# A hybrid decoder trunk: transposes, grams, merges and the recurrence placed at fixed distances among the projections

## The chip, the core and the metric

One Trainium2 chip, one of its cores. The time is the device time of one execution of the whole program in microseconds, of which a median of several runs is given. The matrix engine is TensorE (PE); VectorE (DVE), ScalarE (ACT) and GpSimd (POOL) work elementwise, and SyncE (SP) issues DMAs. Matmuls write to PSUM, which has eight banks, and the elementwise engines empty it.

## What is computed

A trunk of two layers on a sequence of 1024 tokens and 1024 channels, in float32. Each layer is a mixer and a SwiGLU feed-forward part (FFN), each with a norm before and a residual sum after it:

```python
proj = rms_norm(x, norm1_g) @ w_in                 # q, k, v, z of 4 heads, b, a, and 3 x 512 short-conv columns
qkv = silu(causal_depthwise_conv(qkv, dn_conv_w))
q, k = l2_normalize(q), l2_normalize(k)            # 4 heads of 128
beta, g = sigmoid(b_in), -exp(a_log) * softplus(a_in + dt_bias)
o_dn = chunk_gated_delta_rule(q, k, v, g, beta)    # S_t = a_t S_{t-1} (I - b_t k_t k_t^T) + b_t v_t k_t^T, o_t = S_t q_t
o_dn = rms(o_dn) * dn_norm_g * silu(z)
y = gate_b * causal_depthwise_conv(gate_c * hv, sc_conv_w);  o_sc = rms per group(y) * sc_norm_g
x = x + concatenate([o_dn, o_sc]) @ w_out
x = x + (silu(h2 @ ffn_w_gate) * (h2 @ ffn_w_up)) @ ffn_w_down
```

## The kernel before

Tokens lie along the free axis in two halves of 512, channels on the 128 partitions. Each projection of 128 columns and one half is 24 matmuls of 128x512 (mm3, L179 to 184): 8 blocks of channels, each as high part by high part (L182), high by low (L183) and low by high (L184), so that float32 precision is kept with a faster type. ACT makes the high part of a weight (L175), DVE or POOL the low part (L176). All projections share the two PSUM buffers named mm.

The mixer goes head by head. kvq (L432) projects k, q or v of a head and a half; conv_silu (L410 to 427) runs the convolution and the silu on ACT (L418, L420, L426) and DVE (L424, L427) and leaves kT, qT or vT, channels on the partitions. transposed (L451) turns such a tile with four PE transposes into ktok, qtok or vtok, tokens on the partitions. head_stats takes the sums of squares of ktok and qtok and from them the norms and the factors c2, irk and s. prep (L480 to 517) fetches the decay row of a half by DMA (L487), makes eta and the masked exponentials on ACT and POOL (L489 to 499), multiplies the row by c2 on POOL (L500), kdec by kd on DVE (L501), makes v2 from vtok (L504), and the two grams gk and gq (L513), which with the row give U and A (L514); q by eta is POOL's (L515). invert (DVE, 62 steps) and merge (PE products rp and yp, L543 to 580) invert the triangular blocks of 4 tiles of 128 tokens, as X and Y. chain (L584 to 636) is the recurrence over those tiles for two heads: kS = S times k, rr (DVE), TR = Y times rr, vn (ACT), SU and op. zproj and gate apply the silu gate with a transposition ot. sconv makes a short-convolution group and its transposition sp_sc for the sums of squares. ba projects the columns of beta and decay.

The order of work on each engine is not the written order: a list scheduler places the instructions of all engines by their dependencies and its own model of times, with the written order as a priority. A tile's buffers (the dictionary SB, L69) and PSUM banks limit it: a buffer is free when its last reader is done. The row has one buffer, v one, k and q four; in PSUM ch0, ch1, o0, o1, aux and fx have one bank each, mm two. The driver:

```python
head_stats(hd)
for half in range(2):
    if (hd, half) != (0, 0):
        kvq(hd, half, "v")
    prep(hd, half, slots[hd, half])
```

for each head, then invert and all four merges of the pair of heads, then chain for half 0 and half 1, and behind the first pair z of heads 0 and 1 and sconv(0), behind the second sconv 1 to 3 and z of heads 2 and 3. ktok and the merges use the bank aux; qtok ch0; vtok ch1; gk o0; gq o1; ot ch0 and ch1. In the first layer the second half of x is transposed (xtp1) and normed (bc_n1_0_1) ahead of head 0, L291 to 306.

## Time and profile before

| | us |
|---|---|
| median of 3 runs (2547.13 to 2552.06) | 2549.05 |
| the profiled execution's own time | 2534.03 |
| its span | 2532.3 |
| PE busy in it | 2385.5 |
| DVE busy in it | 1666.4 |
| ACT busy in it | 911.6 |
| POOL busy in it | 770.4 |

The busy times are sums over the whole span and do not say which engine sets the end of a stage. The windows of the trace do: they cut the span into stages and give each engine's busy time and the clock granted to PE in each. Positions are in us from the span's start. A row of the waits says which instruction stood still and whose result it stood for; a row of the timeline gives the start and length of an instruction, with the idle time ahead of it in brackets. Ends of matmuls are modelled, so the distance from one start to the next is the better measure of one.

### The profile page before, as it was taken

How to read it: one execution, taken by the hardware profiler on the slowest of the kernel's cores; microseconds unless marked ns; L12 is line 12 of the kernel's file. 1: busy time of each engine (PE TensorE's matmuls, PEld its weight loads, DVE VectorE, ACT ScalarE, POOL GpSimd, SP SyncE). 2: the span in 40 equal slices, each digit the busy share in tenths (PEclk: the TensorE clock that was granted, in tenths of full speed). 3: DMA queues.
4: the chain of work that ended last, by engine and by line, in shares of the span. 5: the costliest groups of instructions: out<-in, count | busy, mean ns of one | idle time of the engine just before them, and what ended most of it. 6: DMA issues, size and time to landing. Idle time of an engine off the chain costs nothing.

```text
span 2532.3 us, 31892 instructions
## 1 busy us (share of the span) xinstructions
PE 2385.5 (94%) x11522; PEld 1935.4 (76%) x11522; DVE 1666.4 (66%) x2771; ACT 911.6 (36%) x1925; POOL 770.4 (30%) x570
## 2 busy tenths in 40 slices
...
GB/s 219 65 56 61 69 57 76 138 202 72 120 100 104 107 102 90 226 137 132 110 76 71 60 55 66 73 63 212 156 77 93 113 116 92 104 147 176 138 130 67
DMA packets 360085, 274.15 MB, mean 108 GB/s; under 512 B 47310, under 2 KB 293368, under 8 KB 359928
## 3 DMA queue, kind: packets, MB, share of 16 engines
...
## 4 chain that ended last, share of the span: by engine, by line
PE 70%; DVE 12%; issue 6%; DMA 5%; ACT 4%; POOL 2%; SPq 0%; POOLq 0%; ACTq 0%; DVEq 0%
PE P_g L183 5%; PE P_g L184 5%; PE P_g L182 5%; PE P_u L183 5%; PE P_u L182 5%; PE P_u L184 5%; PE P_d L183 3%; PE P_d L182 3%; PE P_d L184 3%; DMA row<-gd 2%; PE po L182 2%; PE po L183 2%; PE po L184 2%; PE ps_hsc L182 1%; PE ps_hsc L183 1%
## 5 line engine op out<-in xcount | busy, mean ns | idle before, releaser
L183 PE MATMUL P_g<-lo_hP,hiP_g 128*128 128x512 f32 x616 | 241.6, 393 | 8.6 <-DVE lo_hP L770 6.7
L182 PE MATMUL P_u<-hi_hP,hiP_u 128*128 128x512 f32 x616 | 241.7, 392 | 6.9 <-ACT hiP_u L794 6.9
L182 PE MATMUL P_g<-hi_hP,hiP_g 128*128 128x512 f32 x616 | 240.5, 391 | 1.3 <-ACT hiP_g L794 1.3
L183 PE MATMUL P_u<-lo_hP,hiP_u 128*128 128x512 f32 x616 | 241.4, 392 | 0.0
L184 PE MATMUL P_u<-hi_hP,loP_u 128*128 128x512 f32 x616 | 241.0, 391 | 0.0
L184 PE MATMUL P_g<-hi_hP,loP_g 128*128 128x512 f32 x616 | 240.1, 390 | 0.0
L183 PE MATMUL P_d<-lo_dP,hiP_d 128*128 128x512 f32 x504 | 203.1, 404 | 16.0 <-POOL lo_dP L770 13.0
L182 PE MATMUL P_d<-hi_dP,hiP_d 128*128 128x512 f32 x504 | 202.4, 403 | 11.6 <-ACT hi_dP L769 9.4
L184 PE MATMUL P_d<-hi_dP,loP_d 128*128 128x512 f32 x504 | 199.5, 397 | 1.8 <-DVE loP_d L795 1.7
L1069 DVE TENSOR_TENSOR xT<-P_d,xT 128x512 f32<-128x512 f32 x192 | 127.0, 681 | 53.9 <-PE P_d L184 50.5
L770 POOL TENSOR_TENSOR lo_hP<-xh,hi_hP 128x512 fp32r<-128x512 f32 x24 | 37.1, 1574 | 403.4 <-ACT hi_hP L769 403.4
L183 PEld LDWEIGHTS P_g<-lo_hP,hiP_g 128*128 128x128 f32 x616 | 116.0, 188 | 38.2 <-DVE lo_hP L770 11.1
L182 PEld LDWEIGHTS P_u<-hi_hP,hiP_u 128*128 128x128 f32 x616 | 116.6, 189 | 32.1 <-ACT hiP_u L794 7.8
L182 PEld LDWEIGHTS P_g<-hi_hP,hiP_g 128*128 128x128 f32 x616 | 115.9, 188 | 26.9 <-ACT hiP_g L794 2.1
L184 PEld LDWEIGHTS P_u<-hi_hP,loP_u 128*128 128x128 f32 x616 | 116.6, 189 | 24.5
L183 PEld LDWEIGHTS P_u<-lo_hP,hiP_u 128*128 128x128 f32 x616 | 116.6, 189 | 24.2
L184 PEld LDWEIGHTS P_g<-hi_hP,loP_g 128*128 128x128 f32 x616 | 116.0, 188 | 23.5
L183 PEld LDWEIGHTS P_d<-lo_dP,hiP_d 128*128 128x128 f32 x504 | 97.7, 194 | 44.6 <-POOL lo_dP L770 18.0
L182 PEld LDWEIGHTS P_d<-hi_dP,hiP_d 128*128 128x128 f32 x504 | 97.6, 194 | 38.7 <-ACT hi_dP L769 12.9
L794 ACT CAST hiP_g<-m_g 128x1024 fp32r<-128x1024 f32 (+1 forms) x66 | 60.0, 909 | 175.2 <-PE P_g L183 100.6
L794 ACT CAST hiP_u<-m_u 128x1024 fp32r<-128x1024 f32 (+1 forms) x66 | 60.1, 910 | 170.1 <-PE P_u L183 90.8
L184 PEld LDWEIGHTS P_d<-hi_dP,loP_d 128*128 128x128 f32 x504 | 96.8, 192 | 22.9 <-DVE loP_d L795 3.6
...
## 6 DMA issues: line engine op xcount, KB each, us to landing
stP<-hs_P SPq DMA_DIRECT2D x126, 256.0 KB, 3.8
...
```

The lines of the kernel that those rows point to most:

```text
L182: PE.matmul(ps, lhsT=w(k)[0], rhs=m(k)[0], start=k == 0, stop=False)
L183: PE.matmul(ps, lhsT=w(k)[0], rhs=m(k)[1], start=False, stop=False)
L184: PE.matmul(ps, lhsT=w(k)[1], rhs=m(k)[0], start=False, stop=k == n - 1)
L770: eng.tensor_tensor(res[1], src, res[0].bitcast(F32), ALU.subtract)
L794: S.copy(hi, src)
L1069: V.tensor_tensor(t, ps, t, ALU.add)
```

## The change

Work that is not a projection becomes a job, a generator with a countdown. Every matmul of a projection ticks the countdowns, and a job that comes to 0 is run up to its next yield, which gives the next countdown. The PE instructions that a job issues get an edge that says they are issued after the last projection matmul written so far (issue_after); it is a bound on one side, and the scheduler goes on placing the rest. The distances are constants: 36 matmuls for the transposes, 30 for sp_sc, 12 and 24 in a head's finish, 110 behind invert, 6 between the steps of merge and chain, 10 before a gate.

head_stats and prep are split into key_tok, query_tok, decay, gram and value_tok. decay (the row's DMA, exponentials and mask) is written before v's projection; the row has two buffers and its multiplication by c2 is DVE's. vT lies in a buffer of the z kind. The banks change: ktok, gk, vtok, merges and ot use aux; qtok, gq and sp_sc use fx. The merges of half 1 are written behind the chain of half 0; in the chain the steps of both heads stand together (kS of both, TR of both, SU and op of both). In layer 0 the second half of x is written behind head 0's first three projections, and in both layers v's first weight is loaded and split early, its low part on POOL. The first x tiles lie in other buffers, and their squares come in two parts.

```diff
+LAG, TOK_LAG, SC_LAG, INV_LAG, GATE_LAG = 6, 36, 30, 110, 10
...
-    SB = {"y": 2, "z": 4, "k": 4, "v": 1, "q": 4, "row": 1, "eta": 1, "sqp": 1, "kdec": 4, "v2": 4, "U": 4, "A": 4,
+    SB = {"y": 2, "z": 4, "k": 4, "q": 4, "row": 2, "eta": 1, "sqp": 1, "kdec": 4, "v2": 4, "U": 4, "A": 4,
...
+    def mm3(ps, w, m, n, tick=None):
         for k in range(n):
...
+            for i, j in ((0, 0), (0, 1), (1, 0)):
+                last_mm[0] = PE.matmul(ps, lhsT=w(k)[i], rhs=m(k)[j], start=k + i + j == 0, stop=k + i == n).ins
+                if tick:
+                    tick()
...
-        for c0, name, eng in ((512, f"k{l}_0", G), (0, f"q{l}_0", G)):
+        for c0, name, eng in ((512, f"k{l}_0", G), (0, f"q{l}_0", G), (1024, f"v{l}_0", G)):
...
+    def x_half1():
...
+            jobs = []
+            def spawn(gen, lag=0):
+                jobs.append([lag, gen])
+            def move(job):
+                with tc.issue_after(last_mm[0]):
+                    try:
+                        job[0] = next(job[1])
+                    except StopIteration:
+                        jobs.remove(job)
+            def tick():
+                for job in list(jobs):
+                    job[0] -= 1
+                    if job[0] <= 0:
+                        move(job)
+            def drain():
+                while jobs:
+                    move(min(jobs, key=lambda j: j[0]))
...
-                mm3(ps, wsl(w), lambda k: hs[half][k], KD)
+                mm3(ps, wsl(w), lambda k: hs[half][k], KD, tick)
...
+            def key_tok(hd, half):
...
+                ktok = transposed(u["k"], f"ktok_{nm}", aux)
+                u["kdec"] = sb("kdec", f"kdec_{nm}", sh4)
+                S.copy(u["kdec"], ktok)
+                sumsq(ktok, ss[:, half * 4:half * 4 + 4], f"k_{nm}")
+            def query_tok(hd, half):
...
+                qtok = transposed(units[hd, half]["q"], f"qtok_{nm}", fx)
+                sumsq(qtok, stat(hd)["ss"][:, 8 + half * 4:12 + half * 4], f"q_{nm}")
...
+            def decay(hd, half):
...
                 row = sb("row", f"row_{nm}", sh4)
                 dma(row, dram_ap(gd, (half * 16 + hd) * P, [[0, P], [NH * P, 4], [1, P]]))
...
                 S.activation(eta, row, AF.Exp)
...
                 G.affine_select(out=row, in_=row, compare_op=ALU.is_ge, fill=-1e30, base=0,
...
                     S.activation(row[:, c, :], row[:, c, :], AF.Exp, bias=ngl[:, half * 4 + c, hd:hd + 1])
-                G.tensor_tensor(row, row, c2.unsqueeze(2).broadcast_to(sh4), ALU.mult)
-                V.tensor_tensor(u["kdec"], u["kdec"], kd.unsqueeze(2).broadcast_to(sh4), ALU.mult)
-                vtok = transposed(u["v"], f"vtok_{nm}", bank("ch1"))
...
-                V.scalar_tensor_tensor(v2, vtok, 0.5, u["irk"][:, h4].unsqueeze(2).broadcast_to(sh4),
...
+                u.update(row=row, eta=eta, kd=kd)
...
+            def gram(hd, half, slot):
...
+                V.tensor_tensor(row, row, c2.unsqueeze(2).broadcast_to(sh4), ALU.mult)
...
                 for src, dst in (("k", U), ("q", A)):
-                    gp = ps_({"k": "o0", "q": "o1"}[src], f"g{src}_{nm}", sh4)
+                    gp = ps_({"k": "aux", "q": "fx"}[src], f"g{src}_{nm}", sh4)
...
                     V.tensor_tensor(dst, gp, row, ALU.mult)
-                G.tensor_tensor(u["q"], u["q"], eta.rearrange("p c i -> p (c i)"), ALU.mult)
                 dma(full_ap(ud[slot]), U)
...
+                G.tensor_tensor(u["q"], u["q"], u["eta"].rearrange("p c i -> p (c i)"), ALU.mult)
+                V.tensor_tensor(u["kd"], u["kd"], c2, ALU.mult)
+                V.tensor_tensor(u["kdec"], u["kdec"], u["kd"].unsqueeze(2).broadcast_to(sh4), ALU.mult)
...
+            def value_tok(hd, half):
...
+                vtok = transposed(u["v"], f"vtok_{nm}", aux)
...
+                V.scalar_tensor_tensor(v2, vtok, 0.5, u["irk"][:, h4].unsqueeze(2).broadcast_to(sh4),
+                                       ALU.mult, ALU.mult)
...
+                        cp = chp(hd, "kS", c)
+                        PE.matmul(cp, lhsT=u["k"][:, cs], rhs=state[hd], start=True, stop=True)
...
+                        PE.matmul(op[hd][:, c, :], lhsT=u["q"][:, cs], rhs=state[hd], start=True, stop=False)
+                    if not first:
+                        yield LAG
+                    for hd in hds:
+                        cp = chp(hd, "TR", c)
+                        PE.matmul(cp, lhsT=units[hd, half]["Y"][:, c, :], rhs=rr[hd], start=True, stop=True)
...
+                    yield LAG
+                    for hd in hds:
...
+                            cp = chp(hd, "SU", c)
+                            PE.matmul(cp, lhsT=u["kdec"][:, c, :], rhs=vn[hd], start=True, stop=True)
...
                             state[hd] = Sn
...
+                        PE.matmul(op[hd][:, c, :], lhsT=u["A"][:, c, :], rhs=vn[hd], start=first, stop=True)
+                    if not last:
+                        yield LAG
...
+                yield GATE_LAG
+                for hd in hds:
+                    gate(hd, half)
...
-                ot = transposed(u["on"].rearrange("p c i -> p (c i)"), f"ot_{l}_{hd}_{half}", bank(f"ch{hd % 2}"))
+                ot = transposed(u["on"].rearrange("p c i -> p (c i)"), f"ot_{l}_{hd}_{half}", aux)
...
+                    def stats_job(y=y, half=half, nm=nm):
+                        sumsq(transposed(y, f"sp_{nm}", fx), sc_m[:, g, half * 4:half * 4 + 4], f"_{nm}")
...
+                    spawn(stats_job(), SC_LAG)
...
+            def head(hd, group):
+                order = [(ty, half) for half in range(2) for ty in "kqv"] if hd == 0 else \
+                    [(ty, half) for ty in "kqv" for half in range(2)]
+                for ty, half in order:
+                    if hd == 0 and (ty, half) == ("k", 1):
+                        if l == 0:
+                            hs[1] = x_half1()
                         ba()
-                        for ty in "kq":
-                            kvq(hd, 1, ty)
-                    else:
-                        for ty in "kq":
-                            for half in range(2):
-                                kvq(hd, half, ty)
+                        decay(0, 0)
+                    if ty == "v" and hd + half > 0:
+                        decay(hd, half)
+                    kvq(hd, half, ty)
+                    if ty == "k":
+                        spawn(call(key_tok, hd, half), TOK_LAG)
+                    elif ty == "q":
+                        spawn(call(query_tok, hd, half), TOK_LAG)
+                def finish():
                     head_stats(hd)
+                    yield 12
                     for half in range(2):
-                        if (hd, half) != (0, 0):
-                            kvq(hd, half, "v")
-                        slots[hd, half] = len(slots)
-                        prep(hd, half, slots[hd, half])
+                        gram(hd, half, (hd % 2) * 2 + half)
+                        value_tok(hd, half)
+                        yield 24
+                    if group is not None:
+                        spawn(group, 0)
+                spawn(finish(), TOK_LAG)
+            def group(g):
+                yield 12
                 invert(g)
+                yield INV_LAG
                 for half in range(2):
                     for hd in (2 * g, 2 * g + 1):
-                        merge(hd, half, slots[hd, half])
+                        yield from merge(hd, half, (hd % 2) * 2 + half)
+                    yield LAG
+                    yield from chain(g, half)
+            head(0, None)
+            head(1, group(0))
+            for hd in range(2):
...
                 for half in range(2):
-                    chain(g, half)
-                if g == 0:
-                    for hd in range(2):
...
-                        for half in range(2):
-                            zproj(hd, half, w)
-                    for half in range(2):
-                        for hd in range(2):
-                            gate(hd, half)
-                    sconv(0)
+                    zproj(hd, half, w)
+            sconv(0)
+            head(2, None)
+            head(3, group(1))
             for g in range(1, 4):
                 sconv(g)
-            sc_norm()
+            spawn(call(sc_norm), SC_LAG + 12)
...
             for half in range(2):
                 for i in range(2):
                     zproj(2 + i, half, w[i])
-            for half in range(2):
-                for i in range(2):
-                    gate(2 + i, half)
+            drain()
```

The matmuls of the projections are the same in number, 1376 in each layer's mixer; the changes from a projection to other work on PE go from 96 to 117 in layer 0, and from 92 to 117 in layer 1.

PE at head 1 of layer 0, before: ps_x0_1_h is the projection x of layer 0, head 1, half h; hhi, hlo, hi, lo are the parts of the input and the weight.

```order
L184 MATMUL ps_q0_1_1_1212<-hhi_n1_0_1_7_582,lo_q0_1_1171 128x512
L451 MATMUL ktok_0_1_0_1249<-ident_78,kT_k0_1_0_1119 128x128 x4
L451 MATMUL qtok_0_1_0_1261<-ident_78,qT_q0_1_0_1199 128x128 x4
L182 MATMUL ps_v0_1_0_1323<-hhi_n1_0_0_0_371,hi_v0_1_1319 128x512
...
L184 MATMUL ps_v0_1_0_1323<-hhi_n1_0_0_3_389,lo_v0_1_1320 128x512
L451 MATMUL ktok_0_1_1_1271<-ident_78,kT_k0_1_1_1157 128x128 x4
L182 MATMUL ps_v0_1_0_1323<-hhi_n1_0_0_4_395,hi_v0_1_1319 128x512
...
L184 MATMUL ps_v0_1_1_1402<-hhi_n1_0_1_4_564,lo_v0_1_1320 128x512
L451 MATMUL vtok_0_1_0_1379<-ident_78,vT_v0_1_0_1348 128x128 x4
L182 MATMUL ps_v0_1_1_1402<-hhi_n1_0_1_5_570,hi_v0_1_1319 128x512
```

After:

```order
L186 MATMUL ps_q0_1_0_1158<-hhi_n1_0_0_3_405,lo_q0_1_1155 128x512
L488 MATMUL ktok_0_1_0_1173<-ident_78,kT_k0_1_0_1054 128x128 x4
L186 MATMUL ps_q0_1_0_1158<-hhi_n1_0_0_4_411,hi_q0_1_1154 128x512
...
L186 MATMUL ps_v0_1_0_1305<-hhi_n1_0_0_3_405,lo_v0_1_1302 128x512
L488 MATMUL qtok_0_1_0_1318<-ident_78,qT_q0_1_0_1223 128x128 x4
L186 MATMUL ps_v0_1_0_1305<-hhi_n1_0_0_4_411,hi_v0_1_1301 128x512
...
L564 MATMUL gk_0_1_0_1500<-kT_k0_1_0_1054 128x128 x4
L564 MATMUL gq_0_1_0_1506<-qT_q0_1_0_1223,kT_k0_1_0_1054 128x128 x4
L186 MATMUL ps_z0_1_0_1533<-hhi_n1_0_0_0_387,hi_z0_1_1529 128x512
...
L186 MATMUL ps_z0_1_0_1533<-hlo_n1_0_0_1_394,hi_z0_1_1529 128x512
L488 MATMUL vtok_0_1_0_1516<-ident_78,vT_v0_1_0_1340 128x128 x4
L186 MATMUL ps_z0_1_0_1533<-hhi_n1_0_0_1_393,lo_z0_1_1530 128x512
```

ktok, qtok and vtok stood right behind or in the projection that followed; now each has other projections ahead of it, and gk has moved behind z's.

PE in the chain of heads 0 and 1, layer 0 (the numbers in kS_0_1_0_2 are layer, head, half and tile), before:

```order
L606 MATMUL TR_0_1_0_0_1756<-v2_0_1_0_1384,Y_0_1_0_1607 128x128
L611 MATMUL SU_0_1_0_0_1760<-vn_0_1_0_0_1758,kdec_0_1_0_1254 128x128
...
L601 MATMUL kS_0_1_0_1_1779<-S_0_1_0_0_1762,kT_k0_1_0_1119 128x128
L620 MATMUL op_0_1_0_1746<-S_0_1_0_0_1762,qT_q0_1_0_1199 128x128
L601 MATMUL kS_0_0_0_2_1793<-S_0_0_0_1_1775,kT_k0_0_0_637 128x128
L557 MATMUL rp32_0_0_1_1658<-X_0_0_1_1654,U_0_0_1_1072 32x32
L620 MATMUL op_0_0_0_1745<-S_0_0_0_1_1775,qT_q0_0_0_675 128x128
L606 MATMUL TR_0_1_0_1_1783<-rr_0_1_0_1_1781,Y_0_1_0_1607 128x128
L557 MATMUL rp32_0_0_1_1658<-X_0_0_1_1654,U_0_0_1_1072 32x32 x7
L606 MATMUL TR_0_0_0_2_1797<-rr_0_0_0_2_1795,Y_0_0_0_1561 128x128
L611 MATMUL SU_0_1_0_1_1787<-vn_0_1_0_1_1785,kdec_0_1_0_1254 128x128
```

After:

```order
L677 MATMUL TR_0_0_0_0_2021<-v2_0_0_0_1139,Y_0_0_0_1876 128x128
L186 MATMUL ps_q0_2_1_2225<-hlo_n1_0_1_2_713,hi_q0_2_2131 128x512
L186 MATMUL ps_q0_2_1_2225<-hhi_n1_0_1_2_712,lo_q0_2_2132 128x512
L685 MATMUL SU_0_0_0_0_2049<-vn_0_0_0_0_2023,kdec_0_0_0_555 128x128
L693 MATMUL op_0_0_0_2019<-vn_0_0_0_0_2023,A_0_0_0_1117 128x128
L186 MATMUL ps_q0_2_1_2225<-hhi_n1_0_1_3_718,hi_q0_2_2131 128x512
...
L668 MATMUL kS_0_1_0_1_2080<-S_0_1_0_0_2056,kT_k0_1_0_1054 128x128
L672 MATMUL op_0_1_0_2020<-S_0_1_0_0_2056,qT_q0_1_0_1223 128x128
L668 MATMUL kS_0_0_0_2_2139<-S_0_0_0_1_2107,kT_k0_0_0_484 128x128
L672 MATMUL op_0_0_0_2019<-S_0_0_0_1_2107,qT_q0_0_0_522 128x128
L677 MATMUL TR_0_1_0_1_2095<-rr_0_1_0_1_2082,Y_0_1_0_1940 128x128
L685 MATMUL SU_0_1_0_1_2110<-vn_0_1_0_1_2097,kdec_0_1_0_1178 128x128
```

rp32_0_0_1, of half 1, has left this place; projections of q stand between the first steps, and none between the later ones.

PE at the start of layer 0, where ba is, before:

```order
L184 MATMUL ps_q0_0_0_650<-hhi_n1_0_0_7_413,lo_q0_0_363 128x512
L201 MATMUL bc_n1_0_1_535<-ident_78,rowr_n1_0_1_520 128x128 x4
L182 MATMUL ps_v0_0_0_694<-hhi_n1_0_0_0_371,hi_v0_0_690 128x512
L183 MATMUL ps_v0_0_0_694<-hlo_n1_0_0_0_372,hi_v0_0_690 128x512
L348 MATMUL ba_ps0_0_733<-hhi_n1_0_0_0_371,w_ba0_355 16x512
...
L348 MATMUL ba_ps0_0_733<-hlo_n1_0_0_7_414,w_ba0_355 16x512
L451 MATMUL ktok_0_0_0_902<-ident_78,kT_k0_0_0_637 128x128 x4
L451 MATMUL qtok_0_0_0_914<-ident_78,qT_q0_0_0_675 128x128
L348 MATMUL ba_ps0_1_756<-hhi_n1_0_1_0_540,w_ba0_355 16x512
```

After:

```order
L186 MATMUL ps_v0_0_0_535<-hhi_n1_0_0_3_405,lo_v0_0_379 128x512
L488 MATMUL ktok_0_0_0_550<-ident_78,kT_k0_0_0_484 128x128 x4
L186 MATMUL ps_v0_0_0_535<-hhi_n1_0_0_4_411,hi_v0_0_378 128x512
...
L186 MATMUL ps_v0_0_0_535<-hhi_n1_0_0_7_429,lo_v0_0_379 128x512
L309 MATMUL xtp1_2_1_645<-ident_78,xp_2_1_231 128x128 x4
L309 MATMUL xtp1_3_0_656<-ident_78,xp_3_0_233 128x128 x4
L309 MATMUL xtp1_3_1_667<-ident_78,xp_3_1_235 128x128 x4
L205 MATMUL bc_n1_0_1_695<-ident_78,rowr_n1_0_1_680 128x128 x4
L362 MATMUL ba_ps0_0_757<-hhi_n1_0_0_0_387,w_ba0_367 16x512
...
L362 MATMUL ba_ps0_1_780<-hhi_n1_0_1_0_700,w_ba0_367 16x512
```

The projection of v stands whole ahead of ba, and bc_n1_0_1, the broadcast with which the second half of the input is scaled, stands behind it and behind ktok.

## Rows read from the trace of the kernel before

**Rows 1.** The page: its head, and the chain that ended last, by line.
```profile
span 2532.3 us, 31892 instructions
...
PE P_g L183 5%; PE P_g L184 5%; PE P_g L182 5%; PE P_u L183 5%; PE P_u L182 5%; PE P_u L184 5%; PE P_d L183 3%; PE P_d L182 3%; PE P_d L184 3%; DMA row<-gd 2%; PE po L182 2%; PE po L183 2%; PE po L184 2%; PE ps_hsc L182 1%; PE ps_hsc L183 1%
```

**Rows 2.** Stages of both mixers (windows); the columns stand in the first line.
```profile
core 0: us, PE busy (x) PEld busy (x) DVE busy (x) ACT busy (x) POOL busy (x), PEclk, DMA share, GB/s
...
85.80:144.10 58.30, 47.98 (x240) 39.51 (x238) 44.61 (x88) 27.12 (x77) 13.33 (x12) 0.97 0.27 67
144.10:216.90 72.80, 72.04 (x356) 57.91 (x354) 40.51 (x95) 15.14 (x26) 3.14 (x6) 0.98 0.26 61
216.90:279.80 62.90, 59.23 (x446) 48.37 (x446) 34.69 (x104) 31.20 (x137) 1.49 (x3) 0.86 0.19 54
...
439.00:503.00 64.00, 57.24 (x283) 47.27 (x282) 31.06 (x72) 28.43 (x105) 0.00 (x0) 0.92 0.37 120
...
1326.90:1387.90 61.00, 49.54 (x238) 41.11 (x238) 46.35 (x89) 28.82 (x83) 14.56 (x14) 0.93 0.26 64
...
1461.50:1519.90 58.40, 54.52 (x446) 44.35 (x446) 34.41 (x104) 31.14 (x137) 1.49 (x3) 0.94 0.20 58
```

**Rows 3.** Waits of PE, layer 0's mixer: us in total, times, longest.
```profile
PE vtok L451 <- DVE vT_v L427: 11.1, 5, 4.6
PE qtok L451 <- DVE qT_q L427: 8.8, 2, 4.7
PE ps_v L182 <- ACT hi_v L175: 6.7, 1, 6.7
PE sp_sc L451 <- ACT sq_sc L446: 4.4, 2, 3.4
PE gk L513 <- DVE U L514: 2.4, 2, 1.3
...
PE rp L573 <- DVE Y L570: 1.1, 1, 1.1
```

**Rows 4.** The same waits of layer 1's mixer.
```profile
PE vtok L451 <- DVE vT_v L427: 10.8, 5, 4.3
PE qtok L451 <- DVE qT_q L427: 6.8, 2, 4.3
...
PE ps_k L184 <- POOL lo_k L176: 2.4, 1, 2.4
```

**Rows 5.** Timeline of PE, end of head 1's q (start us, length us).
```profile
116.02 0.72 PE L451 MATMUL qtok<-ident,qT_q 128*128 128x128 f32 x4 [4.01 <-DVE qT_q L427]
...
116.96 0.63 PE L183 MATMUL ps_v<-hlo_n,hi_v 128*128 128x512 f32 x1
117.39 0.63 PE L184 MATMUL ps_v<-hhi_n,lo_v 128*128 128x512 f32 x1
```

**Rows 6.** Timeline of PE, sp_sc in the middle of a projection.
```profile
1592.56 0.39 PE L182 MATMUL ps_csc<-hhi_n,hi_csc 128*128 128x512 f32 x1
1592.79 0.39 PE L183 MATMUL ps_csc<-hlo_n,hi_csc 128*128 128x512 f32 x1
1593.14 0.66 PE L451 MATMUL sp_sc<-ident,y_sc 128*128 128x128 f32 x4
1593.56 0.48 PE L184 MATMUL ps_csc<-hhi_n,lo_csc 128*128 128x512 f32 x1
1593.87 0.40 PE L182 MATMUL ps_csc<-hhi_n,hi_csc 128*128 128x512 f32 x1
```

**Rows 7.** Groups by line, GpSimd: row by c2 (busy us, mean ns).
```profile
L500 POOL TENSOR_TENSOR row<-row,c 128x512 f32<-128x512 f32 x16 | 24.1, 1508 | 33.1 <-DVE s L476 29.1 <-ACT row L499 4.0
```

**Rows 8.** One line, DVE: kdec by kd, shortest/median/longest ns.
```profile
L501 DVE TENSOR_TENSOR kdec<-kdec,kd x16: 676/682/1756, 90.5 to 1576.0; 128x512 f32<-128x512 f32 x16
```

**Rows 9.** Timeline of PE, the first TR of the chain.
```profile
216.92 0.49 PE L606 MATMUL TR<-v,Y 128*128 128x128 f32 x2
```

**Rows 10.** Timeline of ACT, the silu of head 2's second k projection.
```profile
239.10 0.69 ACT L420 ACTIVATE y_k<-ps_k,cst 128x512 f32<-128x512 f32 x1
```

157 lines of the change are left out of this document (81 added, 76 removed).

## The prediction

> **What bounds the kernel now.** I read the page's head and chain first: the span is 2532.3 us, the chain that ended last consists by line of projections and FFN matmuls of TensorE (PE), and the one DMA named in it, row<-gd, has 2% of the span, about 50 us [rows 1]. A kernel so bound gains only where PE stands still or runs at less than full speed, so I read next the stages between the first projection and the out-projection of each layer, the only ones that the change touches [rows 2]. They fall into three kinds. The stages with nothing but z and short-convolution projections are full already, one waits 0.8 us in 72.8. The two head stages of each layer (heads 1 and 3, their projections with transposes and decay rows) are not: 85.80 to 144.10 is 58.30 us long with PE busy for 47.98, 1326.90 to 1387.90 is 61.00 with 49.54. The other two of this kind lie between (11.7 and 10.4 us idle). In the same stages VectorE (DVE) is busy for 44.61 and 46.35 us, so it is the second engine, close behind. The chain stage (recurrence of heads 0 and 1) is 62.90 long with 59.23 busy, at a granted clock of 0.86 of full speed; in layer 1, 58.40 with 54.52 at 0.94. The tail before the out-projection is idle for 6.8 us (6.7 in layer 1).
>
> Then the waits of PE in both mixers [rows 3, 4]. Most is one pattern: vtok waits for vT (11.1 and 10.8 us, 5 times each), qtok for qT (8.8 and 6.8, twice each), sp_sc for the square of the previous one (4.4, and as much in layer 1), ps_v for the split of its weight (6.7, layer 0 only). In each PE reaches a transpose before DVE or ScalarE (ACT) has made its operand, and full-size projections that need nothing stand behind it. At 116.02 qtok starts after 4.01 us of waiting, though its projection had ended about 10 us before; the matmuls behind it then start 0.43 us apart (116.96 to 117.39) [rows 5], where an undisturbed one takes 0.23 (1592.56 to 1592.79) [rows 6]. So a wait costs its length and a stretch at half clock: in 85.80 to 144.10 the 15 slow steps sum to 2.3 us over full speed, 2.2, 2.3 and 1.9 in the other head stages, 2.1 in each tail.
>
> **The change, part by part.** *Transposes and grams at a distance.* Each is put at least 36 matmuls (36 x 0.23 = 8.3 us [rows 6]) behind the projection that feeds it, and a lone wait becomes work. From the end of a projection to kT, qT or vT took 6.3 to 11.2 us in the head stages, with DVE shared among more jobs there than at the new places; so most of it is covered. The whole worth of a head stage is its idle plus its half-clock excess: 12.6 (10.3 + 2.3), 13.9, 13.8 and 12.3 us. DVE's 44 to 46 us leave no room for all of it inside the stage, but the finish of the head (statistics, grams, v2) moves into the stage behind, where DVE is free for a third of the time. I take 10, 11, 10 and 10, with 5 as the low end of each, half of the idle.
>
> *Decay rows.* The row has two buffers and its DMA, exp and select are started before v's projection; in the trace these stand in the chain with 50 us [rows 1], yet PE hides most of it, and what shows is inside the waits of vtok. I give it nothing of its own. The multiplication row by c2 goes from GpSimd (1508 ns each, 16 of them [rows 7]) to DVE. The nearest row there is kdec, same shape and operands: median 682, at most 1756 ns [rows 8]. So DVE gets 8 x 0.68 = 5.5 us more per layer, 1.4 per head, and GpSimd 12 less. It is hidden while PE has covers, and it is in the 10 of 12.6.
>
> The trace shows kdec between 676 and 1756 ns on one shape [rows 8], long where GpSimd runs. The Trainium skill (SBUF — State Buffer, Who interferes with whom) says that a VectorE instruction with two SBUF inputs contends with a GpSimd instruction that reads SBUF; row by c2 is of that kind, and q by eta stays on GpSimd beside it. By that rule every one may take the long time, which the median in this trace does not bear out; what the sum would be is the first rival.
>
> *Chain.* In the trace the first TR stands at 216.92, and the silu of head 2's second k projection starts at 239.10 [rows 9, 10], 22 us later: its buffer is one that the last kS of half 0 has to leave, and the merges of half 1 sit inside that chain. In the new order they come after it, and between the steps stand LAG = 6 matmuls where there are any. Worth in layer 0: 3.7 us of idle and 9.9 us of small matmuls spaced wider than 0.11 us each, so 0 to 13; in layer 1 3.9 and 6.8, 0 to 10. Since the projections still run out in the middle of the chain (the second fence pair of the order shows bare steps in the old one; the new one has some too), I take 6 and 4, under half.
>
> *Tail.* sp_sc stands 30 matmuls (6.9 us) behind its y; that covers the 3.4 us waits [rows 3]. Of 6.8 + 2.1 I take 7 per layer, 4 to 9.
>
> *Start of layer 0.* The early weight split of v removes 6.7 us [rows 3]; the second half of x, now behind the first three projections, makes the second half of ba (the 16 columns of beta and decay) wait instead. That wait is not in the trace; its nearest row is the same 6.7 [rows 3], and with the slow steps of that stage (3.6) the net is 0 to 8. I take 4, the middle. Layer 1 gets nothing here; its 2.4 us for lo_k [rows 4] stay.
>
> Gains: 4 + 10 + 11 + 6 + 7 = 38 in layer 0, 10 + 10 + 4 + 7 = 31 in layer 1, 69 together.
>
> *What it costs.* First, switching: a group of four transposes among projections takes from 1592.79 to 1593.87, less two matmuls of 0.23 and its own 0.42 (1593.14 to 1593.56): 0.2 us more than its work [rows 6]. The order has 21 and 25 such switches more per layer, 46 x 0.2 = 9 us. Second, one PSUM bank, aux, now serves ktok, gk, vtok, the merges and ot: 63 handovers per layer, where ktok and the merges had 39 and the others had banks of their own. Behind gk the next user, vtok, must wait until U is made: about 0.7 us of DVE and its queue, against 0.9 to 1.3 us of cover at five heads' halves. I put 1 us on each such pair, 5 per layer, 10 us together (2 to 20). The chain steps go on sharing ch0 and ch1. Third, the last transposes stand 27 rows (6 us) closer to the out-projection, which may then wait for them. No such wait is in the trace; between 0 and the longest sp_sc wait (3.4 [rows 3]) I take 1.5 per layer, 3 together.
>
> Net: 69 - 22 = 47 us.
>
> **Rivals.** *DVE becomes the bound of the head stages.* With 1.4 us more per head and every transpose due at a set distance, a late DVE makes PE wait at ktok, qtok and gk where it waited at vtok. For it: 44.61 + 1.4 = 46.0 us of DVE against 58.3 - 12.6 = 45.7 of PE in the first [rows 2]. If kdec and row by c2 all took 1.76 us [rows 8], that would be 32 x 1.07 = 34 us more of DVE, 8.6 per stage. Against it: the stage behind has DVE busy for 40.5 of 72.8. Then the head stages give half: 69 - 21 - 22 = 26, so 2523 us.
>
> *Slower: the shared bank.* Each handover of aux is matmul, reader, matmul in turn. In the trace such a turn shows as 1.1 us at rp behind Y [rows 3]. If that were exposed at each of the 63, it would be 63 x 2 x 1.1 = 139 us against 69 - 12 = 57, so 2549 + 82 = 2631; it turns slower from 57 / 126 = 0.45 us per handover. For it: 20 of the 63 have under 1 us of other work between them in the new order. Against it: in the old order 18 of 39 had as little, and PE's waits there are only 1.1 to 2.4 us in all. If half of the handovers showed the 1.1, it is 2549 + 12 = 2561; I take 2575 as the middle of this case.
>
> The Trainium skill (Perfetto Trace Analysis, Matmuls) has it that independent matmul groups should rotate through different PSUM banks, so that emptying one overlaps the next group. The change goes against it with grams and transposes; the 1.1 us row shows that it can cost, and this rival is what it would make of the time.
>
> *The change does not do what it says.* The edges only say "not before that matmul"; a scheduler with its own times still sets the order, and DMA and exp of the row may remain last. Then most waits only change their name, what goes of them is taken back by the 22 us of cost, and the time stays 2549. Against it: the order does show the transposes 12 to 36 matmuls behind.
>
> **How the numbers follow.** The profiled execution took 2534.03 us, 15 under the median of the runs shown (2549.05); 47 us are 1.85% of it, and I take them off the median as they are: 2502. Chances: this forecast 0.66, DVE bound 0.17, no change 0.05, slower by the bank 0.12. About 0.2% (5 us) is what a measurement of this kernel can tell from none. Faster is then 0.83, same 0.05, slower 0.12. Low end: the upper ends of the gains, 8 + 12.6 + 13.9 + 13 + 9 = 56 and 13.8 + 12.3 + 10 + 9 = 45, less 9 + 2 = 11 of cost, give 2459; all at their best at once is unlikely, so two thirds of the way there from 2502, about 2472. High end: DVE bound (2523), plus the upper end of the bank cost (10 more) and the low end of the tails (6 less), is 2539. No change and the slower case, 0.17, are left out.
>
> **What would show it.** Right: in the new profile vtok and qtok are gone from PE's waits, or under 5 us per layer; PE idle for under 4 us in each head stage; few 0.43 us steps outside the chain; the granted clock of the chain stage above 0.9; sp_sc waits under 1 us. The bank would show as vtok, gk, ktok or rp waiting for U, v2, Y or kdec, DVE as ktok and qtok waiting for kT and qT. The start term shows at ba_ps waiting for the lower half of h. Wrong: waits of PE in the mixer of layer 0 that come to over 20 us where the six rows shown now sum to 34.5 [rows 3], or waits on aux over 15 us per layer.

## The result, and the profile after

The changed kernel takes 2457.62 us (2454.18 to 2462.0) where the kernel before takes 2548.09 (2545.35 to 2552.06): a ratio of 0.9645, 95% interval 0.9622 to 0.9667, or 90 us less. On another chip the ratio was 0.9684 (0.9656 to 0.9712). The forecast was 2502, in the right direction, with a range whose low end of 2472 lies above the measured time: the gain was nearly twice what was forecast.

The page of the changed kernel, its head, the clock granted in 40 slices, and the chain by engine:

```profile
span 2453.5 us, 31881 instructions
...
PEclk8999999999999999999999999999999999999999
...
PE 77%; DVE 8%; issue 6%; DMA 3%; ACT 3%; POOL 2%; SPq 1%; POOLq 0%; DVEq 0%; ACTq 0%
```

The span is 78.8 us shorter than the 2532.3 of [rows 1]. The chain that ended last has 77% of PE and no decay row is named in it any more.

All of it lies in the two mixers. I cut both kernels at the same places of the work: first projection, first z projection, first k of head 2, first projection of sconv 1, first z of head 2, first out-projection. Layer 0 before, the first four of these stages (stage, length, busy time and count of PE, PEld, DVE, ACT, POOL, granted clock, DMA share, GB/s):

```profile
24.69:135.46 110.77, 94.73 (x459) 72.57 (x457) 80.29 (x180) 60.89 (x185) 23.26 (x21) 0.94 0.36 101
135.46:197.39 61.93, 57.45 (x251) 46.97 (x250) 41.64 (x94) 13.62 (x26) 5.75 (x9) 0.97 0.31 72
197.39:329.95 132.56, 121.79 (x789) 98.68 (x788) 78.20 (x193) 59.73 (x214) 12.40 (x14) 0.92 0.21 55
329.95:479.19 149.24, 138.15 (x840) 111.76 (x839) 74.02 (x186) 40.93 (x145) 3.69 (x5) 0.95 0.28 73
```

The same after, with the first stage of layer 1 as well:

```profile
25.89:124.52 98.63, 90.23 (x434) 68.66 (x433) 73.47 (x167) 60.10 (x190) 16.62 (x17) 0.97 0.41 117
124.52:184.44 59.92, 59.72 (x286) 49.64 (x284) 45.65 (x114) 16.81 (x36) 4.10 (x6) 1.00 0.26 64
184.44:298.40 113.96, 109.46 (x753) 87.60 (x752) 69.81 (x176) 56.85 (x203) 7.11 (x12) 0.99 0.27 70
298.40:432.48 134.08, 134.08 (x850) 109.56 (x848) 75.29 (x191) 38.37 (x121) 3.76 (x5) 1.00 0.28 73
...
1231.95:1329.97 98.02, 87.92 (x428) 68.99 (x427) 68.28 (x157) 50.32 (x144) 19.39 (x17) 0.98 0.24 64
```

From first projection to out-projection layer 0 went from 478.3 to 433.3 us and layer 1 from 466.8 to 432.8: 45.0 + 34.0 = 79.0. By stage in layer 0: heads 0 and 1 give 12.1, z and sconv 0 2.0, heads 2 and 3 with the first chain 18.6, sconv 1 to 3 with the second chain 15.2, and the last stage takes back 2.9. The reader should look at two columns: PE's busy time has come within 0.2 us of the length in the z and sconv stages, and the clock went from 0.92 to 0.97 up to 0.97 to 1.00. The stage of layer 1 that holds heads 0 and 1 still stands still for 10 us.

The waits of PE after, layer 0 (us in total, times, longest):

```profile
PE vtok L488 <- DVE U L565: 3.0, 2, 2.8
PE ba_ps L362 <- DVE hlo_n L213: 2.9, 3, 1.4
PE ot L488 <- ACT on L709: 1.7, 2, 1.3
PE ba_ps L362 <- POOL hlo_n L213: 1.3, 2, 0.8
PE rp L638 <- DVE Y L634: 1.1, 1, 1.1
```

and layer 1:

```profile
PE vtok L488 <- DVE U L565: 4.8, 2, 4.5
PE ps_k L186 <- POOL lo_k L177: 2.4, 1, 2.4
PE ot L488 <- ACT on L709: 1.7, 2, 1.3
PE ktok L488 <- DVE kT_k L464: 1.6, 1, 1.6
PE bc L205 <- DVE rowr_n L199: 1.3, 1, 1.3
```

Of the waits of [rows 3, 4] those of vtok and qtok for vT and qT, of sp_sc and of ps_v are gone. New are vtok behind U, 3.0 and 4.8 us, which is the shared bank, and ba behind the scaled second half of x, about 4.7 us in all.

Counted over every start of a PE instruction in both mixers, the 79 us are made up about as follows: idle time 78.1 to 28.9 (49 less), full-size matmuls at half clock 19.3 to 7.0 (12 less), the recurrence's small matmuls beyond 0.105 us each 21.4 to 8.6 (13 less), transposes and grams beyond the same 9.7 to -0.3 (10 less), merges 3 less, and the borders between small and full-size work, with the 0.1 us that the second full-size matmul behind a small group loses, 25.1 to 30.6 (5.5 more). The idle time is read from the waits. The other classes depend on which step is put where: they sum to 82 with it, and another division of the same starts gives 11, 10 and 7 for full-size matmuls, the recurrence, and transposes with grams. Each is good to about 3 us.

### The profile page after: what moved, and what is told of

Its sections match the earlier page's. It is cut to its first block, busy times and chain, and to the rows that moved or that the text cites. A ratio compares the mean times of both kernels' runs of the same rounds, so it can differ in the third digit from the quotient of the medians.

```text
span 2453.5 us, 31881 instructions
## 1 busy us (share of the span) xinstructions
PE 2351.7 (96%) x11522; PEld 1908.7 (78%) x11522; DVE 1650.9 (67%) x2786; ACT 915.9 (37%) x1933; POOL 747.2 (30%) x556
## 4 chain that ended last, share of the span: by engine, by line
PE 77%; DVE 8%; issue 6%; DMA 3%; ACT 3%; POOL 2%; SPq 1%; POOLq 0%; DVEq 0%; ACTq 0%
PE P_g L186 16%; PE P_u L186 15%; PE P_d L186 10%; PE po L186 6%; PE ps_csc L186 4%; PE ps_bsc L186 4%; PE ps_hsc L186 4%; PE pd L186 3%; PE ps_q L186 2%; PE ps_v L186 2%; PE ps_z L186 2%; PE ps_k L186 2%; DMA stP<-hs_P 1%; POOL lo_dP L874 1%; DVE lo_hP L874 1%
## 5 line engine op out<-in xcount | busy, mean ns | idle before, releaser
L186 PE MATMUL P_d<-lo_dP,hiP_d 128*128 128x512 f32 x504 | 202.5, 403 | 17.5 <-POOL lo_dP L874 14.6
```

The source lines that it names most:

```text
L186: last_mm[0] = PE.matmul(ps, lhsT=w(k)[i], rhs=m(k)[j], start=k + i + j == 0, stop=k + i == n).ins
```

## Experiments: which part carries the gain

For each kernel the table gives the sum of both mixers in its trace, from first projection to out-projection, which shows a few microseconds that medians don't. Two traces of one kernel differ by 5.7 us (before) and 2.8 us (changed), so smaller differences say nothing. With them stand the median and the ratio to the kernel before on the same chip, where it was timed.

| kernel | both mixers, us | median, us | ratio (95%) |
|---|---|---|---|
| before | 945.1 | 2548.09 | 1 |
| before, traced again | 950.8 | | |
| changed | 866.1 | 2457.62 | 0.9645 (0.9622 to 0.9667) |
| changed, again | 868.9 | 2458.51 | 0.9684 (0.9656 to 0.9712) |
| e2, no distance | 868.1 | 2459.59 | 0.9688 (0.9662 to 0.9714) |
| e14, buffers undone | 867.4 | 2460.76 | 0.9693 (0.9666 to 0.9720) |
| e20, both of these undone | 893.8 | 2480.65 | 0.9781 (0.9750 to 0.9811) |
| e17, chain undivided | 881.0 | 2470.44 | 0.9739 (0.9709 to 0.9770) |
| e21, chain at once | 947.7 | 2536.73 | 0.9998 (0.9981 to 1.0014) |
| e22, e20 and e21 | 951.9 | | |
| e8, start undone | 874.6 | | |
| e3, old banks | 852.6 | 2444.22 | 0.9624 (0.9600 to 0.9648) |
| e10, all on aux | 883.6 | 2475.42 | 0.9745 (0.9721 to 0.9770) |
| e5, v first | 879.4 | 2469.06 | 0.9723 (0.9693 to 0.9754) |
| e12, before with the buffers | 920.9 | 2502.42 | 0.9861 (0.9837 to 0.9885) |
| e15, that with a late finish | 937.0 | 2518.87 | 0.9922 (0.9892 to 0.9951) |
| e7, before with merges split | 954.8 | 2538.58 | 0.9998 (0.9982 to 1.0014) |
| e23, before with the chain as a job | 906.7 | 2488.35 | 0.9803 (0.9759 to 0.9846) |
| e24, that with the buffers | 899.3 | 2482.18 | 0.9776 (0.9726 to 0.9826) |
| e19, changed with old banks and more | 851.0 | 2439.88 | 0.9616 (0.9590 to 0.9643) |

### The distances and the edges

```diff
-LAG, TOK_LAG, SC_LAG, INV_LAG, GATE_LAG = 6, 36, 30, 110, 10
+LAG, TOK_LAG, SC_LAG, INV_LAG, GATE_LAG = 6, 1, 1, 110, 10
```

> The changed kernel with the distances of the transposes (36) and of sp_sc (30) set to 1; jobs, banks, decay rows and the chain's order stay. Theory D (the written distance is what covers the 6 to 11 us from a projection's end to kT, qT and vT): PE idle for ktok, qtok, vtok and sp_sc comes back, 10 to 20 us per layer, and with it half-clock steps: 2480 to 2500 us. Rival S (it is enough that the jobs are separate pieces, so that the scheduler spreads them by itself): within 0.4% of the changed kernel, 2448 to 2467 us, and PE idle in the mixers as in the changed kernel, 13.5 and 15.4 us.

Rival S: 868.1 against 866.1 us, idle 12.4 and 11.0 us in the two mixers. The written distance of 36 and 30 matmuls, on which the prediction rested its cover, is worth nothing by itself. The distances inside a head's finish (12 and 24), behind invert (110) and ahead of a gate (10) were not varied. The edges are worth nothing either: the changed kernel written without them comes out as the same program, instruction for instruction.

### The buffers

In the kernel before alone, and undone in the changed one (here the first; the second is its reverse):

```diff
-    SB = {"y": 2, "z": 4, "k": 4, "v": 1, "q": 4, "row": 1, "eta": 1, ...
+    SB = {"y": 2, "z": 4, "k": 4, "q": 4, "row": 2, "eta": 1, ...
...
-                dst = sb(ty, f"{ty}T_{nm}")
+                dst = sb({"v": "z"}.get(ty, ty), f"{ty}T_{nm}")
```

> The kernel before with the changed buffers alone: two for the decay row, vT in the four of the z kind. Theory M (one buffer for the row and one for vT made the waits, since half 1 has to wait until half 0 has used them): vtok's waits halve, 20 to 35 us off the 945 us of both mixers. Theory L (the waits come from where a head's finish is written, right behind its projections): under 8 us, vtok and qtok wait as before.

> The changed kernel with one buffer for the row and one of its own for vT, as before. Theory M: 20 us or more are lost of the 79 that both mixers gained in the profiles. Theory L: 0 to 8 us, since a late finish has time for the row of half 0 and half 1 in turn.

Theory M for the kernel before, by 24 us in the trace, and nothing (1.3 us) for the changed one. Why it is so much alone can be read in the DVE queue of the kernel before. With one row buffer, the row of half 1 can only be fetched when A, the last reader of half 0's row, has run; one row of DVE's timeline and the DMA in the chain of waits:

```profile
102.30 0.68 DVE L514 TENSOR_TENSOR A<-gq,row 128x512 f32<-128x512 f32 x1
...
107.88 0.17 DVE L490 COPY gl<-eta 128x4 f32<-128x4 f32 x1 [1.66 <-ACT eta L489]
```

```profile
103.05 4.05 DMA row<-gd
```

A begins at 102.30, the DMA lands 4.05 us after 103.05, and gl, behind eta, holds DVE for 1.66 us at 107.88, with the conv of head 1's k queued behind it. From the end of a projection to its finished kT and qT, head 1 of layer 0 took 10.8, 11.3, 10.0 and 9.8 us; with the buffers alone 6.5, 6.2, 5.2 and 6.0. The waits of PE in layer 0 with the buffers alone:

```profile
PE vtok L451 <- DVE vT_v L427: 7.6, 3, 3.5
...
PE qtok L451 <- DVE qT_q L427: 1.3, 1, 1.3
```

qtok's 8.8 us [rows 3] are 1.3, without any transpose moved. The buffer for the row and the one for vT were not tried apart. In DVE's waits of the kernel before, layer 0, it is the row that shows:

```profile
DVE kd L492 <- DMA row<-gd: 7.7, 5, 2.5
...
DVE gl L490 <- ACT eta L489: 5.2, 5, 2.4
```

With the buffers these are 1.5 and 3.6 us, and no wait of DVE for a free vT is among them in either kernel, so the row is the likelier of the two. So there seem to be two cures for the same waits: a shorter way to qT, and work in the meantime. That was tested by taking both away.

> The changed kernel with both undone: the distances of transposes and sp_sc set to 1, and one buffer each for the row and for vT. Each alone changed the two mixers by under 2 us (868 and 867 us against 866). Theory R (either cure suffices: two row buffers shorten the way from a projection's end to kT, qT and vT to about 6 us, the distance covers 8): together undone they cost 15 to 30 us, 2470 to 2490, and the way to qT and vT is 8 to 15 us again with waits of vtok and qtok. Rival (neither matters, it is the jobs' order alone): within 5 us of the changed kernel.

The cost is theory R's: 893.8 us, 28 more than the changed kernel, though each undone alone cost 1 to 2. Its signs are there only in part. kT, qT and vT of head 1 come 11.7, 16.6, 8.4, 5.5, 5.9 and 7.3 us behind their projections, where the changed kernel has about 7.7, 11.8, 8.0, 5.8, 5.1 and 7.5, so only the way to kT grew. PE waits in layer 0 for kT and on the shared bank:

```profile
PE vtok L488 <- DVE U L565: 6.9, 5, 2.5
PE ktok L488 <- DVE kT_k L464: 4.9, 3, 2.8
```

Most of the loss lies behind the heads: in layer 0 z and sconv 0 take 5.2 us more (65.10) and sconv 1 to 3 6.9 more (140.99). Why the two together cost so much there stays open; that they do is what the runs show.

### The chain as a job

```diff
                     if group is not None:
-                        spawn(group, 0)
+                        for _ in group:
+                            pass
```

> The changed kernel with invert, merges and chain of a pair of heads written in one go where the head's finish ends, ahead of sconv 1 to 3, instead of as a job that goes on between projections. Theory C: the scheduler then places the chain of heads 2 and 3 as bare small matmuls with three sp_sc right behind it, as in the kernel before, and the stage of sconv 1 to 3 goes from 134 to 142 to 150 us in each layer, that of heads 2 and 3 from 114 to 118 to 125: 20 to 50 us in all. Rival: PE is as busy with bare small matmuls as with mixed ones, under 8 us.

Theory C, beyond its range: 82 us, the whole gain and a little more. The stages of heads 2 and 3 and of sconv 1 to 3, layer 0:

```profile
188.03:312.31 124.28, 115.17 (x753) 91.20 (x752) 73.33 (x177) 58.62 (x212) 7.38 (x12) 0.93 0.25 64
312.31:477.35 165.04, 150.11 (x870) 122.64 (x869) 78.31 (x204) 42.70 (x146) 3.76 (x5) 0.91 0.24 65
```

124.28 and 165.04 us, where the changed kernel has 113.96 and 134.08, and a clock of 0.93 and 0.91 instead of 0.99 and 1.00. The timeline of PE there shows why:

```profile
446.38 0.49 PE L668 MATMUL kS<-S,kT_k 128*128 128x128 f32 x2
446.70 0.39 PE L672 MATMUL op<-S,qT_q 128*128 128x128 f32 x2
447.31 0.49 PE L677 MATMUL TR<-rr,Y 128*128 128x128 f32 x2 [0.22 <-DVE rr L670]
448.21 0.49 PE L693 MATMUL op<-vn,A 128*128 128x128 f32 x2 [0.41 <-ACT vn L679]
451.10 0.66 PE L488 MATMUL sp_sc<-ident,y_sc 128*128 128x128 f32 x4 [2.40 <-ACT sq_sc L483]
```

From 405 to 448 us steps of the recurrence and merges follow one another with no projection between them, the last ones wait for the engine that makes their operand, and sp_sc, with 2.40 us more, stands behind the block. In the changed kernel a full-size matmul stands between the steps:

```profile
391.58 0.38 PE L668 MATMUL kS<-S,kT_k 128*128 128x128 f32 x2
391.80 0.39 PE L672 MATMUL op<-S,qT_q 128*128 128x128 f32 x2
391.94 0.48 PE L186 MATMUL ps_csc<-hlo_n,hi_csc 128*128 128x512 f32 x1
```

The written order is the scheduler's priority: what is written in one block ahead of sconv 1 to 3 is taken as soon as it is ready, and three sp_sc are left for the end. The other way round, built up from the kernel before, with that part alone, then with the buffers:

```diff
-                invert(g)
-                for half in range(2):
-                    for hd in (2 * g, 2 * g + 1):
-                        merge(hd, half, slots[hd, half])
-                for half in range(2):
-                    chain(g, half)
+                spawn(group(g, slots))
```

> The kernel before with one part of the change alone: invert, merges, chain and gates of a pair of heads as a job among the projections (the changed kernel's own distances in it, edges too); a head's finish, buffers, banks, sp_sc and the start as before. Theory C (the written place of the chain carries the largest part): the stage of sconv 1 to 3 goes from 149 to 134 to 140 us in each layer, without any distance of sp_sc, and the stage of heads 2 and 3 from about 130 to 115 to 125; 30 to 55 us in all, the head stages' waits of vtok and qtok stay. Rival: the chain as a job helps only together with the late finish, under 15 us.

> The same with the changed buffers as well (two for the row, vT in the z kind). Theory: the two cures are of different stages and add up: 20 to 35 us more than the chain as a job alone, so within 20 us of the changed kernel, 2450 to 2480 us. Rival: the finish in parts behind other projections is needed too, and more than 25 us are missing to the changed kernel.

The job alone gives 38 us, with these stages in layer 0:

```profile
198.08:318.07 119.99, 114.45 (x789) 92.83 (x788) 76.90 (x193) 58.47 (x206) 10.92 (x14) 0.99 0.23 63
318.07:456.91 138.84, 135.28 (x831) 108.50 (x830) 72.66 (x186) 40.77 (x145) 3.48 (x5) 0.99 0.29 78
```

It brings the clock of the chain stage from 0.92 to 0.99, and sp_sc's waits in layer 0 from 7.1 to 1.6 us, with sp_sc written just where it was. The waits of vtok (8.9 us) and qtok (7.1) stay, as expected. With the buffers it is 46 us, 7 more and not the 20 to 35 expected. 33 us are then missing to the changed kernel, the number that the rival of that run named. Where they are missing can be read by stage (layer 0's sconv 1 to 3 with the second chain, layer 1's heads 0 and 1, layer 1's heads 2 and 3):

```profile
315.37:449.28 133.91, 133.51 (x832) 107.13 (x830) 70.69 (x182) 39.09 (x138) 1.83 (x3) 1.00 0.29 78
...
1245.07:1353.55 108.48, 97.54 (x464) 77.58 (x463) 80.27 (x177) 53.91 (x151) 23.78 (x22) 0.92 0.23 62
1411.47:1534.10 122.63, 115.70 (x789) 94.47 (x788) 79.09 (x196) 61.00 (x211) 12.56 (x16) 0.97 0.23 62
```

The sconv stage is the changed kernel's already (134.08). The head stages are 10.5 and 8.6 us longer than the changed kernel's in layer 1, where undoing the new start costs about 1 us (below), and 13.6 and 8.6 in layer 0. What the changed kernel has there besides is the finish in parts behind other projections, with it the early decay rows, the multiplication by c2 on DVE, the distances, and the banks, which cost it. No run adds one of these alone to this kernel, so that it is the finish is likely and not shown. A late finish was tried undivided, in plain written order:

> The kernel before with the changed buffers, and with the finish of heads 0, 1 and 2 (head_stats and prep, undivided, in plain written order, no jobs, no distances) written behind the k projections or z of the next; head 3, the chain and the tail as before. Theory L: the stage of heads 0 and 1 loses most of its waits, as in the changed kernel: from 110.8 to under 103 us in layer 0, z and sconv 0 from 61.9 to about 60; 15 to 30 us of the 79. Rival: the parts must be divided and spread, then the waits of ktok, qtok and vtok only move behind z, and the gain is under 8 us.

```diff
+                for half in range(2):
+                    kvq(b, half, "k")
+                finish(a)
```

This kernel also has the first pair's merges and chain written behind z and sconv 0, which its expectation does not say. Heads 0 and 1 take 99.8 us instead of 112.7 with the buffers alone, and the next stage 63.1 instead of 56.6, as the work of head 1's finish has moved there: PE's waits for other engines' results are 0.9 us in it, so the rival's waits did not move behind z. Over these two stages the late finish wins 6.4 us in layer 0. What it loses, it loses in the tail with its bare chain, which grew from 140.7 to 155.9. Why the tail grew was not tested. Two parts of the chain's change by themselves:

> The kernel before with one part alone: the merges of half 1 are written behind the chain of half 0. Theory L: the stage of heads 2 and 3 with the chain loses 3 to 8 us in each layer (buffers of k come free earlier, fewer bare small matmuls), and the granted clock there rises from 0.92 to 0.95 or more; the rest stays. Rival: merges and chain keep filling the same stretch in another order, under 2 us.

```diff
                         merge(hd, half, slots[hd, half])
-                for half in range(2):
                     chain(g, half)
```

> The changed kernel with merges and chain as one piece each of the written order (no yields of 6 between their steps), all else as it is. Theory C (the pieces make the chain run among projections): bare small matmuls at half clock come back, 5 to 12 us in each layer's stage of heads 2 and 3 and in that of sconv 1 to 3. Rival: what puts projections between is that the finish and the chain are written after them at all, the steps need not be apart: within 4 us of the changed kernel's 433 us per mixer.

One of its places, where the yields between steps go:

```diff
-                    yield LAG
                     for hd in hds:
                         cp = chp(hd, "TR", c)
```

Moving the merges of half 1 behind the chain of half 0 is worth nothing (954.8 against 945.1 and 950.8); the prediction had put the chain's gain down to it. Yielding between the steps is worth 15 us (881.0 against 866.1).

All three undone at once:

> The changed kernel with distances, buffers and the chain as a job undone at once; banks, the start of layer 0, the parts of a head's finish and their place behind other projections stay. If the three make up the gain, the two mixers sum to 920 to 945 us (before 945, changed 866); what is missing to 945 is the worth of the finish in parts and of the start.

951.9, which is 4 us more than with the chain at once alone and less than two traces of one kernel differ by: the costs overlap, and the late finish, the start and the new banks together then win nothing over the kernel before. By stage they do win and lose: in layer 0 heads 0 and 1 take 100.61 us (before 110.77) and heads 2 and 3 123.76 (132.56), but z and sconv 0 65.11 (61.93) and sconv 1 to 3 161.03 (149.24). What is won in the heads is lost behind them, most of it where the bare chain is.

### The banks

> The changed kernel with the PSUM banks of the kernel before for the grams (o0, o1), qtok (ch0) and vtok (ch1); ot stays on aux. Theory P (a shared bank costs only where it shows as idle: vtok behind U, 2.8 and 4.8 us in the mixers of the two layers): those waits go, some waits for the chain's banks come, 2448 to 2460 us. Rival B (each handover of aux costs some tenths of a us even where no idle shows): 2400 to 2440 us, since half of the 126 handovers go.

```diff
-                    gp = ps_({"k": "aux", "q": "fx"}[src], f"g{src}_{nm}", sh4)
+                    gp = ps_({"k": "o0", "q": "o1"}[src], f"g{src}_{nm}", sh4)
```

(likewise qtok to ch0, vtok to ch1.) Theory P's number was missed on the good side: 13.5 us less in the mixers, the waits of vtok for U gone, idle 9.1 and 10.1 us. Not half of the 126 handovers of aux went but 32 (gk and vtok, 8 of each in a layer), and as many left fx (qtok and gq). If those of fx are worth nothing, it is 0.42 us each.

> The changed kernel with qtok, gq and sp_sc moved from the bank fx to aux as well, 48 handovers of aux more in the two layers. Theory P: a handover costs only where under 1 us of other work lies between; gq behind gk (16 of them) does, so up to 16 x 0.7 = 11 us if nothing is put between, less since the order puts projections there: 2458 to 2470 us. Rival B (0.45 us or more for each): 22 us or more, 2480 us and up.

```diff
-                    gp = ps_({"k": "aux", "q": "fx"}[src], f"g{src}_{nm}", sh4)
+                    gp = ps_({"k": "aux", "q": "aux"}[src], f"g{src}_{nm}", sh4)
```

(likewise qtok and sp from fx to aux.)

17.5 us more for 48 handovers, 0.36 each, between the two theories. Against the second trace of the changed kernel the two prices are 0.51 and 0.31, so 0.3 to 0.5 us is what can be said. PE's waits in layer 0 then name the bank:

```profile
PE ktok L488 <- DVE v L578: 2.2, 3, 1.4
...
PE gq L564 <- DVE U L565: 2.1, 2, 1.3
```

The Trainium skill (Perfetto Trace Analysis, Matmuls) would have matmul groups rotate through different banks; both runs agree with it, at about 0.4 us for each handover moved. The orders differ by some rows too, so that is no pure price of a bank.

> The changed kernel with vtok and v2 written ahead of row by c2 and the grams. Theory P: vtok needs only irk and leaves aux after one DVE instruction (0.68 us), so the waits of vtok for U (2.8 and 4.8 us) shrink to at most 1 us of gk for v2 each: 2449 to 2455 us. Rival: DVE's queue is what is late there, then gk or gq waits the same 7 us for v2 or U and the time stays at 2457.

```diff
-                        gram(hd, half, (hd % 2) * 2 + half)
                         value_tok(hd, half)
+                        gram(hd, half, (hd % 2) * 2 + half)
```

Neither: 13 us slower. The wait moved and did not shrink, as the rival said, and a lower clock came on top (0.92 in the stage of heads 0 and 1 of layer 0, 0.97 in the changed kernel):

```profile
PE gk L564 <- DVE v L578: 4.6, 2, 2.6
```

DVE takes v2 late because its queue is full: ahead of the longer of these waits it works without a pause from the end of vtok (95.1 us) to v2 (98.71). What stands second on the bank waits for that.

### The start, and a better version

> The changed kernel with the start of layer 0 as before: the second half of x ahead of head 0, v's first weight split when v comes. The prediction gave the start 4 us (0 to 8): layer 0's mixer is 4 us longer, layer 1's the same within 2 us. If the wait of ba for the scaled half and that of v for its split are worth the same, no difference.

```diff
-        for c0, name, eng in ((512, f"k{l}_0", G), (0, f"q{l}_0", G), (1024, f"v{l}_0", G)):
+        for c0, name, eng in ((512, f"k{l}_0", G), (0, f"q{l}_0", G)):
...
-    h1 = None
+    h1 = x_half1()
```

Layer 0 is 7.1 us longer than in the changed kernel, 4.9 than in its second trace, and layer 1 1.4 or 0.8: the start is worth 5 to 7, inside the 0 to 8.

> The changed kernel with the old banks for grams, qtok and vtok, with the low part of k's first weight in layer 1 on DVE, and with the second half of x written ahead of head 0 again, while v's early split stays. Theory: the waits of vtok for U (7.6 us in both layers), of ps_k for lo_k (2.4) and of ba for the scaled half (5.2, and some slow steps) go, 15 to 25 us less than the changed kernel beside it. Rival: as in the kernel before, the scaling on DVE stands ahead of head 0's silu, and PE waits for kT and v instead: 8 to 14 us less, what the banks alone give.

```diff
-        for c0, name, eng in ((512, f"k{l}_0", G), (0, f"q{l}_0", G), (1024, f"v{l}_0", G)):
+        for c0, name, eng in ((512, f"k{l}_0", V if l else G), (0, f"q{l}_0", G), (1024, f"v{l}_0", G)):
...
-    h1 = None
+    h1 = x_half1()
```

(with the banks of e3.) Faster than the changed kernel beside it on the same chip, 2439.88 against 2458.51 us, and the intervals of their ratios (0.9590 to 0.9643, 0.9656 to 0.9712) do not meet. Nearly all of that is the banks (851.0 against 852.6 with these alone): ba no longer waits, but a ktok waits 3.9 us for kT, as the rival had it. It is the fastest kernel of this study.

### The kernel before, again

> The kernel before once more, for its trace alone: where its executions differ. If the difference between 2534 us (the profiled execution shown) and the medians of 2539 to 2549 is half-clock time behind PE's waits, a longer execution has the same waits within 2 us and a lower granted clock.

> The changed kernel once more, on one chip with the next ones. Its executions scatter less than those of the kernel before, since fewer of its matmuls run at half clock: granted clock 0.978 to 0.986, 2450 to 2462 us.

The second trace of the kernel before was as quick as the first (2534.33 us, clock 0.971, vtok 11.2 and qtok 8.8 us), so no execution near the median was seen from inside. But the times and clocks of its timed executions go together: on one chip from 2530.7 us at a clock of 0.971 to 2548.1 at 0.962. The changed kernel's profiled executions stood at 0.982 and 0.985.

## Why the prediction was wrong in size

It was right about where the time lay: PE waited where DVE had not finished, ran at half clock behind it, and gained when other work stood there. The signs that it named are there: vtok and qtok no longer wait for vT and qT, sp_sc waits for nothing, the clock of the chain stage is 0.99. It was wrong about what would win that time. The written distances, on which it rested the head stages and the tail (41 + 14 of its 69 us), are worth 2 us by themselves, and the part that carries most, the chain as a job, had 10 us. That the direction came out owes much to the change holding more than the prediction saw in it. The steps one by one:

**The gains, taken at 69 of 101.** With the costs measured below, the 79 us of the traces mean about 99 us of gain: the upper ends, whole. I took 10 or 11 of each head stage because DVE had 44 to 46 us of its own there. The stage behind had room: of the 10.3 to 11.7 us of idle 1.6 to 4.5 are left (heads 1 and 3 of both layers), most of it vtok behind U, which is the bank. The first rival, DVE as the bound, did not happen: DVE is busy for 45.65 of 59.92 us in the z stage after, PE for 59.72.

**The chain and the tail, 6 + 4 and 7 + 7.** This is the step that failed most, in its reason and in its size. I read the tail's waits as sp_sc standing too near its y, and priced a distance of 30 matmuls; the distance is worth nothing, and the waits came from the second chain, written in one block ahead of sconv 1 to 3 (the job for both chains is worth 82 us when undone, 38 when done alone). I gave the first chain its gain for the merges' order, which is worth nothing; it comes from the job and its pieces. These stages, the last one's loss of 2.9 included, gave 30.9 and 25.2 us, after all costs, in the layers where head 3, chain and tail stand at 24 and 21 before them.

**What is beyond 0.105 us in transposes and grams.** In the head stages I counted the half clock on full-size matmuls alone. Small ones behind a wait lose too, and gave 7 to 10 us in both mixers that stand in no term.

**The decay rows, nothing of their own.** Right for the sum, since the distances cover the same waits (1.3 us when undone), and wrong as a reading: with vT's buffer they are worth 24 us in the kernel before, because the wait for the row's DMA stood in DVE's queue and so in the way to the next head's kT and qT. I had the 6 to 11 us of that way as a fixed length to be covered; for head 1 some 4 of 10 us were queue.

**The costs, 22.** Nearly right in sum and less so in parts: switching 9, measured 5.5 at the borders; the shared bank 10, measured 13.5; the end 3, where rt_sc waits 1.2 (0.8 before). The start's 4 was 5 to 7. The multiplication by c2 on DVE took what was said:

```profile
L557 DVE TENSOR_TENSOR row<-row,c x16: 680/690/694, 94.3 to 1521.4; 128x512 f32<-128x512 f32 x16
```

What I missed is what it took off DVE. I set the median against the long kdec [rows 8]. By the start times it is a rule: in the kernel before six of the 16 took 1011 to 1756 ns, and each of them began while an instruction of GpSimd was running. One of them, with q by eta on GpSimd:

```profile
139.70 1.70 POOL L515 TENSOR_TENSOR qT_q<-qT_q,eta 128x512 f32<-128x512 f32 x1
...
140.19 1.75 DVE L501 TENSOR_TENSOR kdec<-kdec,kd 128x512 f32<-128x512 f32 x1
```

GpSimd is done at 141.40, and kdec 0.54 us later; the ten with no GpSimd instruction running took 676 to 691 ns. In all twenty traces it is the same: the 68 kdec and row by c2 of over 900 ns lasted for the rest of a running GpSimd instruction and some 0.55 us more, and the 460 others took 672 to 695 ns. The Trainium skill (SBUF — State Buffer, Who interferes with whom) holds that a VectorE instruction with two inputs in SBUF contends with a GpSimd one that reads SBUF; the trace agrees. With row by c2 gone from GpSimd, DVE's kdec, kT, qT, vT and the steps of their convolutions run 2 to 3 us over their usual lengths in both mixers, where it was 16 to 17 before (two traces each). So the multiplication cost DVE 11 us and took about as much off it. No run moved it by itself, so what that is worth to PE is not shown.

**The second rival,** the bank, decided from 0.45 us for all 126 handovers, with 57 us to lose. 0.3 to 0.5 was measured on those that were moved, and the gain to lose was 99. The change is faster, and it gave away the 13.5 us that the old banks bring.

**From one execution to the median.** I took the difference of the profiled execution off the median as it was. The median gained 90.5, the traces 78.8: the kernel before loses 15 us more in a usual execution than in the profiled one (2549.05 against 2534.03), the changed one 2. By the clocks listed above that goes with a lower granted clock. Since no such execution was traced, where in it those microseconds lie stays open.
